# Activation tables loaded at other places, two sums of squares on VectorE, normalised tiles spread over more products, and stores of low parts written one weight later

## The chip, the cores and the metric

One core of one Trainium2 chip runs the whole kernel. The metric is the device time of one launch in microseconds (us), the median of several runs. Its engines are called here as the profile calls them: PE is TensorE (matrix products), DVE is VectorE, ACT is ScalarE, POOL is GpSimd, and SP is SyncE, whose queue issues most of the DMA transfers. Each engine works through its own list of instructions in order.

## The reference, cut to what matters

One layer of a streaming encoder over 1056 frames (1024 of a prompt, 32 of a sample) of 1024 features:

```python
x = x + (sigmoid(ga) * a + sigmoid(gb) * bo) @ w_mix_out      # gated mixers; bo = (...) @ w_conv_out
hc = rms_norm(x, g_cross)
cq = (hc @ w_cq).reshape(B, n, MEM_HEADS, MEM_HEAD_DIM)
s = jnp.einsum('bqhd,bmhd->bhqm', cq, mem_k) * MEM_SCALE
p = jax.nn.softmax(s, axis=-1)
co = jnp.einsum('bhqm,bmhd->bqhd', p, mem_v).reshape(B, n, MEM_DIM)
x = x + co @ w_co
hm = rms_norm(x, g_mlp)
x = x + jnp.square(jax.nn.relu(hm @ w_up)) @ w_down
y = rms_norm(x, g_final)
```

`rms_norm` divides by the root of the mean square of a frame's features, so ACT needs its square root table for each norm and its exponential table for each softmax. Everything is float32.

## The kernel before, in words

**Layout.** Features lie on the 128 partitions in eight blocks (`f` = 0 to 7), frames along the free dimension in three chunks (`CH`): chunk 0 and 1 have 384 frames, chunk 2 has 288. A block of a chunk is one tile.

**Products.** Each float32 operand is split into a high part (rounded, by ACT) and a low part (the rest, by DVE), and a product is the sum of three matmuls: high by high, high by low, low by high (`gemm`, lines 200 to 202; in the MLP lines 885 to 887 and 1817 to 1819). Results collect in PSUM in tiles called `acc`, of which there are three, so a product can start only when the one three before it has been read out. In the MLP's last part another pool of such banks is used, also called `acc` in the profile.

**Weights.** `next_w` hands a product its weight; weights are prepared in the order of `worder`, two ahead (`LOOK`). `fetch_w` (line 159) loads one into `wr`, `issue_w` splits it into `wh` (ACT, line 129) and `wl` (DVE, line 130). Eight weights that serve several chunks are in `kept`: at the first use their low part is stored to DRAM (`wl_d`, line 179), and at later uses it is loaded back (line 172) in place of the DVE split.

**Norms.** `square_acc` squares each tile on ACT (line 279) and adds it to `xacc` on POOL (line 281). `chunk_col` sums over the partitions with matmuls into `pq` (line 232) and finishes on ACT (a square root, line 239) and DVE. `chunk_row` spreads the result over the frames: three products with the identity on ACT and DVE (lines 251 and 252), two matmuls into `pr` (lines 253 and 254), and a copy to `R[c]` on ACT (line 264).

**The middle stage,** about 830 to 1140 us of the span, runs the rest of the mixer, cross-attention and the start of the MLP of different chunks beside each other. For chunk `c`: `do_conv_out(c, f)` eight times (its `acc` read by DVE at line 1073, an addition on POOL at line 1074, a split into `M` tiles by line 129 and 130), `do_mix(c, f)` eight times (each sums over all eight `M` tiles; line 1088 and 285), `do_cq(c, j)` twice (line 1137, and 1141 and 1142 for the queries `Y`), the heads of `Cross` (`scores`: line 1168, exponentials at 1173, division at 1174 and 1176; `turn`: transposes at 1185 and splits into `PTh` and `PTl`; `values`: line 1204 to 1219), and `do_co(c, half)` twice (lines 1231 to 1235). Then `normed(c, f)` makes the MLP's input: a DVE multiply by gain and `R[c]` (line 1310), a store to `xn_d` by SP (line 1313), and for chunk 0 a high part on ACT (line 1321) and a low part on DVE (line 1322).

**Order.** `fillers` is the list of products of chunk 2 and of the first MLP products; `then(i, ...)` puts the steps of the chunk that is one stage on behind filler `i`. Fillers 0 to 7 are `do_conv_out(2, f)`, `do_mix(2, f)` come from 8 on with three `up_one` products between them. From this order a scheduler at build time makes each engine's list, moving instructions by its own estimate of when they can run; what is wrapped in `pin` keeps its order. Loads of ACT's tables are put in where a function of another table comes next in ACT's list.

**The end.** The MLP's last products add into the residual tiles (`to_x1`, line 1801), `squares_of` squares finished tiles, `final(0)` and `final(1)` write the output of the first chunks (line 1842 and 1843), and `final_last(2)` transposes chunk 2 on PE (line 1857), takes `chunk_col(2)` and scales out of PSUM (lines 1872 and 1874).

Of the kernel before, what the change touches and what calls it, by code (L numbers as in the profile page):

```python
# [18 lines left out]
P = 128  # L19
# [21 lines left out]
def hybrid_step(ctx: ExitStack, tc: tile.TileContext, io):  # L41
# [5 lines left out]
    def nm(s):  # L47
        uid[0] += 1
        return f"{s}_{uid[0]}"
# [91 lines left out]
            src = src[j]  # L141
        return src

    fetched = []
    third = {}

    def fetch_w(raw=None):
# [16 lines left out]
    def issue_w(pieces=(slice(0, 1024),)):  # L164
        if not fetched:
            fetch_w()
        raw = fetched.pop(0)
        key = worder[wpos[0]]
        hi = wp.tile([P, 1024], F32R, tag="wh", name=nm("wh"))
        lo = wp.tile([P, 1024], F32R, tag="wl", name=nm("wl"))  # L170
        if kept.get(key) is not None:
            sp.dma_start(lo.bitcast(F32), kept[key])
            act.copy(hi, raw)
        else:
            for at in pieces:
                split(hi[:, at], lo[:, at], raw[:, at])
            if key in kept:
                kept[key] = dram.tile([P, 1024], F32, name=nm("wl_d"))
                sp.dma_start(kept[key], lo.bitcast(F32))
        ready.append((worder[wpos[0]], (hi, lo)))  # L180
        wpos[0] += 1

# [62 lines left out]
    def stats_row(blocks, n, rcol):  # L245

        pr = ps.tile([P, n], F32, tag="pt", bufs=2, name=nm("pr"))
        dh, dl = tmp(n, F32R), tmp(n, F32R)
        for j, b in enumerate(blocks):
            s, r, eye = slice(j * P, b + P), rcol[:, j : j + 1], ident[:, j * P - b :]  # L250
            act.mul(dh[:, s], eye, r)
            dve.scalar_tensor_tensor(dl[:, s], eye, r, dh[:, s].bitcast(F32), op0=ALU.mult, op1=ALU.subtract)
        pe.matmul(pr, ones_r, dh, start=True, stop=False)
        pe.matmul(pr, ones_r, dl, start=False, stop=True)
        return pr
# [2 lines left out]
        RC[c] = misc.tile([P, 3], F32, tag=f"rc{c}", name=nm("rc"))  # L258
        stats_col(accs[c], BLOCKS[c], RC[c], pinned)

    def chunk_row(c):
        n = CH[c][1]
        R[c] = misc.tile([P, n], F32, tag=f"R{c}", name=nm("R"))
        act.copy(R[c], stats_row(BLOCKS[c], n, RC[c]))

    def chunk_stats(c):
        chunk_col(c)
        chunk_row(c)

    def square_acc(x, f, c, on_pool=False):  # L270
        n = CH[c][1]
# [28 lines left out]
    def norm_x():  # L300
# [3 lines left out]
            pe.matmul(acc_tile([P, 384]), spin[:, :P], spin, start=True, stop=True)  # L304
        pool_e.memset(ones, 1.0)
        first_raw = wp.tile([P, 1024], F32, tag="wr", bufs=2, name=nm("wr"))
        warm = misc.tile([P, 1], F32, name="warm")
        with tc.manual_schedule(engines={mybir.EngineType.Activation}):
            act.dma_start(prm, io["params"])
            act.dma_start(first_raw[:, :256], weight(worder[0])[:, :256])  # L310
            act.activation(warm, ones, AF.Sqrt)
        make_identity(nc, ident)
        raws = []

# [814 lines left out]
    def do_cq(c, j):  # L1129
        def fn(w):  # L1130
            n = CH[c][1]
            a = acc_tile([P, n])
            gemm(a, w, xc[c])
            if c == j == 0:
                chunk_row(c)
            t = tmp(n)
            dve.scalar_tensor_tensor(t, a, 0.125, R[c], op0=ALU.mult, op1=ALU.mult)
            for e in range(2):
                own, other = slice(64 * e, 64 * e + 64), slice(64 - 64 * e, 128 - 64 * e)
                q = yslot(c)  # L1140
                act.copy(q[own], t[own])
                dve.tensor_sub(q[other], t[own], q[own].bitcast(F32))
                qc[2 * j + e, c] = q

        return fn
# [106 lines left out]
    def open_first():  # L1252

        closed(m_cm)
        S["l"] = ctx.enter_context(tc.tile_pool(name="first", bufs=4, reuse_waits="tile"))
        S["z"] = ctx.enter_context(tc.tile_pool(name="second", bufs=8, reuse_waits="tile"))
        for f in range(NF):
            z = zslot()
            xa[1][f] = (quarter(z, 0), quarter(z, 1))
            pool_e.dma_start(xa[1][f][1].bitcast(F32)[:, : CH[0][1] - QT], xn_d[:, f, QT : CH[0][1]])  # L1260
        for name in ("w_cq", "w_co"):
            del kept[name, 1]

    def open_sums():
        closed(cr_cm)
# [452 lines left out]
    def then(i, *what):  # L1718
        at.setdefault(i, []).extend(what)
# [1 line left out]
    call = lambda fn, *args: lambda: item(lambda: fn(*args))  # L1721
    assert len(left) == 1
    then(0, *[call(x) for x in left[0][1]])
    then(1, call(chunk_stats, 1))
    then(2, *[lambda j=j: item(do_cq(1, j), ("w_cq", j)) for j in range(2)])
    for f in range(NF):
        then(f // 2, call(normed, 0, f))
    for i, (_, calls) in zip((3, 5, 7, 9, 11, 12), cross_units(1)):
        then(i, *[call(x) for x in calls])
    then(14, lambda: item(do_co(1, 0), ("w_co", 0)))  # L1730
# [6 lines left out]
        then(19 + f // 4, call(normed, 1, f))  # L1737
        then(21 + f // 4, call(second_split, f))
    then(19, call(chunk_col, 2))
    then(20, call(chunk_row, 2))  # L1740
    then(21, lambda: item(do_cq(2, 0), ("w_cq", 0)))
    then(22, lambda: item(do_cq(2, 1), ("w_cq", 1)))
    for i, (_, calls) in zip((23, 25, 26, 28, 29, 31, 32), cross_units(2)):
        then(i, *[call(x) for x in calls])
    then(33, call(open_sums))
    then(34, lambda: item(do_co(2, 0), ("w_co", 0)))
    then(35, lambda: item(do_co(2, 1), ("w_co", 1)))
    for k in range(4):
# [36 lines left out]

    def squares_of(c, x):

        if c == 2 and done[c] == NF - 1:
            sq = tmp(CH[c][1])
            act.activation(sq, x, AF.Square)  # L1790
            accs[c].append(sq)
        else:
            square_acc(x, done[c], c)
        done[c] += 1
# [236 lines left out]
```

## Time and profile before

| | us |
|---|---|
| median of three runs | 1740.44 |
| the three runs | 1740.31, 1743.03, 1740.44 |
| the profiled execution, its own time | 1743.76 |
| span of the profiled execution (first to last instruction) | 1742.0 |
| DVE busy in the span | 1192.8 (68%) |
| ACT busy | 852.9 (49%) |
| POOL busy | 588.0 (34%) |
| mean DMA rate | 199 GB/s |

The span is what the profile covers; the profiled execution's own time is 1.76 us longer than it. In the rows of the profile, a name such as `ct` stands for any tile of that name. "L1073" is line 1073 of the kernel before. "[1.81 <-ACT S L1173]" behind a row says that the engine sat idle for 1.81 us before it, and what ended that. A matmul's record is longer than the spacing of matmuls, since they are pipelined; rows of other engines may also overlap by about 0.1 us. Thirteen table loads stand in ACT's list.

### The profile page before, as it was taken

The page shows a single profiled execution, that of the slowest core. Times are in us where ns is not written, and L with a number is a line of the kernel's source. Part 1 is how long each engine was busy: PE and PEld are TensorE (multiplying, and loading weights), DVE is VectorE, ACT ScalarE, POOL GpSimd, SP SyncE. Part 2 cuts the span into 40 slices and gives each one's busy share as a digit, 9 for nine tenths or more (in the row PEclk, how much of TensorE's full clock was granted, in tenths as well). Part 3 has the DMA queues.
Part 4 walks back from the last instruction along what each step waited for, and adds up shares of the span by engine and source line. Part 5 has one row for each costly group of instructions (what it writes and reads, how often), then busy time and mean ns, then how long its engine had stood idle before and what let it go on. Part 6 is the DMA issues. An engine that isn't in the chain of part 4 may idle for free.

```text
span 1742.0 us, 32567 instructions
## 1 busy us (share of the span) xinstructions
PE 1722.9 (99%) x12238; PEld 1706.9 (98%) x12238; DVE 1192.8 (68%) x2278; ACT 852.9 (49%) x1660; POOL 588.0 (34%) x669
## 2 busy tenths in 40 slices
PE   9999999999999999999999999999999999999998
PEld 8999999999999999999999999999999999999998
DVE  7776776867666756555677888787666686545675
ACT  8653533535335324434556666765444553333443
POOL 0026366453643444442225142106555410000121
PEclk9999999999999999999999999999999999999999
DMA  4333344333435888867766667686666695555554
GB/s 186 103 125 127 117 134 146 121 135 131 159 132 199 296 300 291 290 200 244 265 218 200 223 221 249 222 271 199 214 224 217 218 324 182 193 188 173 189 171 161
DMA packets 179853, 346.60 MB, mean 199 GB/s; under 512 B 18656, under 2 KB 101248, under 8 KB 179568
## 3 DMA queue, kind: packets, MB, share of 16 engines
q1 hardware_dynamic: 163504, 290.07, 50.3%
q0 software_dynamic: 15568, 53.68, 9.0%
q8 instruction: 96, 1.57, 0.4%
q10 hardware_dynamic: 624, 0.77, 0.1%
q14 instruction: 61, 0.50, 0.1%
HBM read 250.73 MB, written 93.14 MB: 197 GB/s over the span
## 4 chain that ended last, share of the span: by engine, by line
PE 55%; DMA 3%; DVE 2%; ACT 1%; issue 1%; POOLq 0%; POOL 0%; DVEq 0%; ACTq 0%; SPq 0%
PE acc L885 6%; PE acc L886 6%; PE acc L887 6%; PE acc L1817 5%; PE acc L1819 5%; PE acc L1818 5%; PE acc L200 4%; PE acc L202 4%; PE acc L201 4%; PE pc L885 2%; PE pc L887 2%; PE pc L886 2%; DMA wr<-wsum_d 1%; DVE wl L130 1%; PE pa L202 1%
## 5 line engine op out<-in xcount | busy, mean ns | idle before, releaser
L129 ACT CAST wh<-wr 128x1024 fp32r<-128x1024 f32 (+1 forms) x214 | 223.8, 1046 | 363.4 <-PE acc L1818 125.5
L130 DVE TENSOR_TENSOR wl<-wr,wh 128x1024 fp32r<-128x1024 f32 (+1 forms) x214 | 277.8, 1298 | 109.5 <-ACT wh L129 108.7
L200 PE MATMUL acc<-X,wh 128*128 128x384 f32 (+1 forms) x864 | 281.4, 326 | 0.0
L201 PE MATMUL acc<-X,wh 128*128 128x384 f32 (+1 forms) x864 | 278.6, 322 | 0.0
L202 PE MATMUL acc<-X,wl 128*128 128x384 f32 (+1 forms) x864 | 277.8, 322 | 0.0
L281 POOL TENSOR_TENSOR xacc<-xacc,ct 128x384 f32<-128x384 f32 (+1 forms) x58 | 77.5, 1339 | 384.6 <-ACT ct L279 382.8
L201 PEld LDWEIGHTS acc<-X,wh 128*128 128x128 f32 x864 | 162.7, 188 | 1.2 <-DVE X L285 0.2
L200 PEld LDWEIGHTS acc<-X,wh 128*128 128x128 f32 x864 | 162.4, 188 | 0.8
L202 PEld LDWEIGHTS acc<-X,wl 128*128 128x128 f32 x864 | 162.4, 188 | 0.1
L200 PE MATMUL acc<-Y,wh 128*128 128x384 f32 (+1 forms) x432 | 139.4, 324 | 3.5 <-DVE ct L1073 3.0
L202 PE MATMUL acc<-Y,wl 128*128 128x384 f32 (+1 forms) x432 | 139.2, 323 | 1.4 <-DMA wl<-wl_d 1.4
L201 PE MATMUL acc<-Y,wh 128*128 128x384 f32 (+1 forms) x432 | 139.1, 322 | 0.0
L129 ACT CAST PTh<-pt 128x512 fp32r<-128x512 f32 (+3 forms) x94 | 45.9, 517 | 113.3 <-PE pt L603 111.5
L1817 PE MATMUL acc<-n,wh 128*128 128x264 f32 x352 | 100.3, 285 | 0.0
L1818 PE MATMUL acc<-n,wh 128*128 128x264 f32 x352 | 100.1, 284 | 0.0
L1819 PE MATMUL acc<-n,wl 128*128 128x264 f32 x352 | 99.9, 284 | 0.0
L740 POOL TENSOR_TENSOR ws<-ws 128x256 f32<-128x256 f32 x100 | 88.7, 887 | 5.6
L740 POOL TENSOR_TENSOR xacc<-xacc 128x256 f32<-128x256 f32 x100 | 87.7, 877 | 5.7 <-DMA xacc<-in_w_in 0.4
L200 PEld LDWEIGHTS acc<-Y,wh 128*128 128x128 f32 x432 | 80.8, 188 | 4.8 <-DVE ct L1073 3.9
L202 PEld LDWEIGHTS acc<-Y,wl 128*128 128x128 f32 x432 | 81.1, 188 | 1.8 <-DMA wl<-wl_d 1.8
L201 PEld LDWEIGHTS acc<-Y,wh 128*128 128x128 f32 x432 | 81.1, 188 | 0.0
L589 ACT ACTIVATE S<-S,nmx 128x257 f32<-128x257 f32 (+1 forms) x132 | 64.2, 488 | 18.9 <-DVE nmx L584 18.5
(433 smaller groups left out, 5544.5 us busy)
## 6 DMA issues: line engine op xcount, KB each, us to landing
wr<-in_w_up SPq DMA_DIRECT2D x53, 512.0 KB, 4.7
wr<-in_w_in SPq DMA_DIRECT2D x52, 512.0 KB, 3.6
wr<-wsum_d SPq DMA_DIRECT2D x40, 512.0 KB, 3.5
wr<-in_w_conv_out SPq DMA_DIRECT2D x24, 512.0 KB, 3.9
wr<-in_w_mix SPq DMA_DIRECT2D x24, 512.0 KB, 4.8
wr<-in_w_down SPq DMA_DIRECT2D x24, 512.0 KB, 3.6
n_d<-Z SPq DMA_DIRECT2D x32, 264.0 KB, 4.1
xacc<-in_w_down POOLq DMA_DIRECT2D x16, 512.0 KB, 4.6
```

Of the source, the lines that this page charges most:

```text
L129: act.copy(hi, src)
L130: dve.tensor_sub(lo, src, hi.bitcast(F32))
L200: pe.matmul(out, wh[:, a], hi, start=(k == 0), stop=False)
L201: pe.matmul(out, wh[:, a], lo, start=False, stop=False)
L202: pe.matmul(out, wl[:, a], hi, start=False, stop=(k == len(acts) - 1))
L740: pin(pool_e.tensor_tensor(t[:, to], t[:, x], t[:, y], op=ALU.add))
L885: pe.matmul(acc, wh[:, a], hi, start=(start and k == 0), stop=False, skip_group_check=True)
L886: pe.matmul(acc, wh[:, a], lo, start=False, stop=False, skip_group_check=True)
L887: pe.matmul(acc, wl[:, a], hi, start=False, stop=(k == 3), skip_group_check=True)
L1817: pe.matmul(a, wh[:, s], hi, start=(t == 0 and k == 0), stop=False, skip_group_check=True)
L1818: pe.matmul(a, wh[:, s], lo, start=False, stop=False, skip_group_check=True)
L1819: pe.matmul(a, wl[:, s], hi, start=False, stop=(t == 1 and k == 7), skip_group_check=True)
```

## The change

1. **Tables.** `chunk_row` can take a table: behind the copy of `R[c]` ACT runs one dummy activation of one column with scale 0 into `warm`, so that the load of the exponential table stands there and not ahead of the first softmax of that chunk's cross-attention. This is done for all three chunks. `root_table`, called at filler 33 behind `open_sums`, does the same with the square root once the last exponential of chunk 2 is over; it reads the last attention tile, so it comes behind its writing. The number of table loads stays thirteen.
2. **Last squares.** In `squares_of`, the squares of the last two finished tiles of chunk 2 go into tiles of their own on ACT. The first is appended to the list of sums, and DVE adds the second to it. Before, only the last had its own tile, and POOL added the one ahead of it to `xacc`.
3. **Normalised tiles.** `normed(0, f)` stood at fillers 0 to 3, two at each; it now stands at fillers 1 to 8, one at each.
4. **Stores.** The store of a kept weight's low part is written in the code when the next weight is issued (list `leaving`), not at once.

```diff
@@ issue_w
         hi = wp.tile([P, 1024], F32R, tag="wh", name=nm("wh"))
         lo = wp.tile([P, 1024], F32R, tag="wl", name=nm("wl"))
+        for to, at in leaving:
+            sp.dma_start(to, at.bitcast(F32))
+        leaving.clear()
...
                 kept[key] = dram.tile([P, 1024], F32, name=nm("wl_d"))
-                sp.dma_start(kept[key], lo.bitcast(F32))
+                leaving.append((kept[key], lo))
...
-    def chunk_row(c):
+    warm = []
+
+    def chunk_row(c, table=None):
         n = CH[c][1]
         R[c] = misc.tile([P, n], F32, tag=f"R{c}", name=nm("R"))
         act.copy(R[c], stats_row(BLOCKS[c], n, RC[c]))
+        if table:
+            act.activation(warm[0], R[c][:, :1], table, scale=0.0)
...
             if c == j == 0:
-                chunk_row(c)
+                chunk_row(c, AF.Exp)
...
+    def root_table():
+        act.activation(warm[0], co[2][1][0][:, :1].bitcast(F32), AF.Sqrt, scale=0.0)
...
-    then(1, call(chunk_stats, 1))
+    then(1, call(chunk_stats, 1, AF.Exp))
...
     for f in range(NF):
-        then(f // 2, call(normed, 0, f))
+        then(1 + f, call(normed, 0, f))
...
-    then(20, call(chunk_row, 2))
+    then(20, call(chunk_row, 2, AF.Exp))
...
-    then(33, call(open_sums))
+    then(33, call(open_sums), call(root_table))
...
     def squares_of(c, x):
 
-        if c == 2 and done[c] == NF - 1:
+        if c == 2 and done[c] >= NF - 2:
             sq = tmp(CH[c][1])
             act.activation(sq, x, AF.Square)
-            accs[c].append(sq)
+            if done[c] == NF - 2:
+                accs[c].append(sq)
+            else:
+                dve.tensor_add(accs[c][1], accs[c][1], sq)
```

Lines of the kernel after the change are 3 to 13 higher than before.

**DVE, from the norm of chunk 0 to the first normalised tiles.** The rows are DVE's list behind the `rc` of chunk 0; `ct` from `acc` and `Ga` is the reading of a `do_conv_out(2, f)` product, `ct` from `Ga`, `prm` and `R` is the first half of a `normed`, `Y` from `ct` its second half. Before:

```order
L252 SCALAR_TENSOR_TENSOR ct_11242<-ident,rc_11224,ct_11241 128x128 x3
L130 TENSOR_TENSOR wl_11391<-wr_2080_11388,wh_11390 128x1024
L238 TENSOR_SCALAR st_v_11311<-pq_11307 128x3
L1310 SCALAR_TENSOR_TENSOR ct_11252<-Ga_1703_9819,prm,R_11239 128x384
L240 RECIPROCAL st_y_11313<-st_s_11312 128x3
L241 TENSOR_TENSOR st_t_11314<-st_v_11311,st_y_11313 128x3
L242 SCALAR_TENSOR_TENSOR st_t_11314<-st_t_11314,st_y_11313 128x3
L1322 TENSOR_TENSOR Y_2044_11256<-ct_11252,Y_2043_11255 128x264
L1310 SCALAR_TENSOR_TENSOR ct_11259<-Ga_1715_9868,prm,R_11239 128x384
L1073 TENSOR_TENSOR ct_11299<-acc_11274,Ga_1385_8179 128x288
```

Now, at the same place:

```order
L255 SCALAR_TENSOR_TENSOR ct_11243<-ident,rc_11225,ct_11242 128x128
L1080 TENSOR_TENSOR ct_11286<-acc_11261,Ga_1385_8179 128x288
L255 SCALAR_TENSOR_TENSOR ct_11243<-ident,rc_11225,ct_11242 128x128 x2
L130 TENSOR_TENSOR wl_11372<-wr_2071_11369,wh_11371 128x1024
L241 TENSOR_SCALAR st_v_11298<-pq_11294 128x3
L130 TENSOR_TENSOR M_11290<-ct_11286,M_11289 128x288
L243 RECIPROCAL st_y_11300<-st_s_11299 128x3
```

The reading of the second `do_conv_out` product (from `Ga_1385`) was the tenth of these rows and is the second; the first normalised tile has moved behind the whole norm of chunk 1.

**ACT, about the last table load of the middle stage.** `lt` from `acc` is the reading of an `up` product, `Y` and `h` from `tO` the end of the last attention head, `n` and `t` from `ct` are casts of MLP operands, `st_s` the root. Before, the two places read:

```order
L1213 CAST Y_2458_13049<-tO_13425 64x256
L1218 CAST h_2541_13429<-tO_13425 64x256
L1385 ACTIVATE lt_13599<-acc_13522 128x264
L129 CAST wh_13552<-wr_2581_13550 128x1024
```

```order
L1404 CAST t_2545_13468<-ct_13729 128x240
L1404 CAST n_2553_13479<-ct_13730 128x240
L239 ACT_TABLE_LOAD
L239 ACTIVATE st_s_13757<-st_v_13756 128x3
L1385 ACTIVATE lt_13767<-acc_13700 128x264
```

Now:

```order
L1220 CAST Y_2458_13052<-tO_13428 64x256
L1225 CAST h_2541_13432<-tO_13428 64x256
L1272 ACT_TABLE_LOAD
L1272 ACTIVATE warm<-Y_2458_13052 128x1
L1395 ACTIVATE lt_13603<-acc_13526 128x264
L129 CAST wh_13556<-wr_2581_13554 128x1024
```

```order
L1414 CAST t_2545_13471<-ct_13733 128x240
L1414 CAST n_2553_13479<-ct_13734 128x240
L242 ACTIVATE st_s_13761<-st_v_13760 128x3
L1395 ACTIVATE lt_13771<-acc_13704 128x264
```

The load has left the place ahead of the root and stands, with the dummy, 22 rows earlier, ahead of another reading of an `up` product.

**SP, about a store of a low part.** `wl_d` from `wl` is the store, `wl` from `wl_d` a load of another low part, `wr` the loads of weights. Before:

```order
L179 DMA wl_d_10275<-wl_10272 128x1024
L159 DMA wr_10402<-in_w_conv_out 128x1024
L159 DMA wr_10461<-in_w_conv_out 128x1024
L159 DMA wr_1862_10501<-in_w_mix 128x1024
L1069 DMA ct_10408<-m_d_93 128x384
L159 DMA wr_10576<-in_w_mix 128x1024
L172 DMA wl_10464<-wl_d_9596 128x1024
```

Now:

```order
L172 DMA wl_d_10275<-wl_10272 128x1024
L159 DMA wr_10403<-in_w_conv_out 128x1024
L159 DMA wr_10462<-in_w_conv_out 128x1024
L159 DMA wr_1862_10502<-in_w_mix 128x1024
L1076 DMA ct_10409<-m_d_93 128x384
L159 DMA wr_10577<-in_w_mix 128x1024
L175 DMA wl_10465<-wl_d_9596 128x1024
```

Nothing has moved but line numbers and names; the same holds of all eight stores, and of SP's whole list up to the second `do_conv_out` of chunk 2.

More of the change, by code (lines that the diff above doesn't have):

```diff
@@ L142, in weight @@
         return src
-    fetched = []
+    fetched, leaving = [], []
     third = {}
@@ L264, in chunk_row, with chunk_stats @@
         act.copy(R[c], stats_row(BLOCKS[c], n, RC[c]))
-    def chunk_stats(c):
+        if table:
+            act.activation(warm[0], R[c][:, :1], table, scale=0.0)
+    def chunk_stats(c, table=None):
         chunk_col(c)
-        chunk_row(c)
+        chunk_row(c, table)
     def square_acc(x, f, c, on_pool=False):
@@ L306, in norm_x @@
         first_raw = wp.tile([P, 1024], F32, tag="wr", bufs=2, name=nm("wr"))
-        warm = misc.tile([P, 1], F32, name="warm")
+        warm.append(misc.tile([P, 1], F32, name="warm"))
         with tc.manual_schedule(engines={mybir.EngineType.Activation}):
@@ L310, in norm_x @@
             act.dma_start(first_raw[:, :256], weight(worder[0])[:, :256])
-            act.activation(warm, ones, AF.Sqrt)
+            act.activation(warm[0], ones, AF.Sqrt)
         make_identity(nc, ident)
@@ L1134, in fn @@
             if c == j == 0:
-                chunk_row(c)
+                chunk_row(c, AF.Exp)
             t = tmp(n)
```

## The prediction

> **What bounds the kernel now.** First the page's opening rows (engine, busy us, share of the span, instructions), then PE's waits: the engine, what it was to write and at which line, what released it, and total, times and longest.
>
> ```profile
> span 1742.0 us, 32567 instructions
> PE 1722.9 (99%) x12238; PEld 1706.9 (98%) x12238; DVE 1192.8 (68%) x2278; ACT 852.9 (49%) x1660; POOL 588.0 (34%) x669
> ...
> PE acc L200 <- DVE ct L1073: 3.0, 3, 1.5
> PE acc L886 <- DVE Z L1328: 1.8, 2, 0.9
> PE acc L202 <- DMA wl<-wl_d: 1.4, 1, 1.4
> PE acc L304 <- DVE ct L302: 1.3, 1, 1.3
> PE acc L885 <- ACT lt L1385: 1.2, 1, 1.2
> PE pq L232 <- POOL xacc L281: 0.9, 1, 0.9
> PE acc L885 <- DVE Gb L1235: 0.8, 1, 0.8
> ```
>
> PE is busy 99% of the span and the change takes no product away. So the stake is PE's idle time, and these seven rows make 10.4 us of it: no step can win more than its own row. Four touch the change: the three waits for line 1073 (a bank `acc` that DVE reads late), the wait for the low part from `wl_d`, the wait for `lt` at line 1385, and the wait for POOL's last addition. A second sort of loss shows in the windows (stretch, its length, busy us and count of PE, PEld, DVE, ACT and POOL, granted clock, DMA share and rate):
>
> ```profile
> 1074.00:1076.00 2.00, 2.00 (x11) 2.00 (x10) 1.87 (x5) 1.22 (x3) 0.00 (x0) 0.50 0.52 189
> ...
> 1078.00:1080.00 2.00, 2.00 (x19) 2.00 (x18) 1.57 (x5) 2.00 (x5) 0.00 (x0) 1.00 0.00 0
> ```
>
> PE counts as busy in both, but at a clock of 0.50 it gets 11 matmuls done instead of 19. Eight matmuls in 2 us are some 0.8 us; the whole dip, about twice as long, I estimate at 1.7. It stands right behind the two waits for line 1328.
>
> **The change part by part: stores.** All eight stores stay at the same row of SP's list, as the order rows show, so the wait for `wl_d` (1.4) stays: 0. Bounds 0 and 0.
>
> **The square root's load.** Before, ACT did this:
>
> ```profile
> 1119.51 0.39 ACT L1385 ACTIVATE lt<-acc 128x264 f32<-128x264 f32 x1 [0.29 <-PE acc L887]
> 1120.85 1.05 ACT L129 CAST wh<-wr 128x1024 fp32r<-128x1024 f32 x1 [0.95 <-PE acc L886]
> ...
> 1135.46 1.28 ACT L239 ACT_TABLE_LOAD   x1
> 1136.75 0.20 ACT L239 ACTIVATE st_s<-st_v 128x3 f32<-128x3 f32 x1
> 1136.87 0.37 ACT L1385 ACTIVATE lt<-acc 128x264 f32<-128x264 f32 x1
> ```
>
> The load held back `lt`, and PE waited 1.2 for it. Without it `lt` is 1.28 earlier and the wait goes. What is late next is the `lt` of 1119.51: 1.28 for the load and 0.20 for a dummy stand ahead of it. ACT idles 0.29 and 0.95 there, so 1.48 − 1.24 = 0.24 us reach the `wh` behind it, which is prepared ahead. I take 1.1 of the 1.2. Bounds: 0, if PE waits as long for the delayed `lt`, and 1.2.
>
> The Trainium skill, "ScalarE: Activation LUTs", section "What ACT_TABLE_LOAD costs", puts a switch at a load of 1283 ns and a drain of 1380 ns. The 1.28 agrees, but here the next instruction starts 0.01 us behind the load's end, with no drain; by the page this gain would shrink by up to 1.4. The rows decide.
>
> **Tables for the softmax.** Chunk 0's load moves from about 894 to 887 us, where PE has no wait: 0, bounds 0 and −0.2 for the dummy. Chunk 1's belongs to the next part. Chunk 2's moves from 1083.91, where PE doesn't wait either, to behind the first of the three casts here:
>
> ```profile
> 1071.12 1.04 ACT L1327 CAST Z<-Z 128x264 fp32r<-128x264 f32 x3
> ...
> 1072.87 1.11 DVE L1328 TENSOR_TENSOR Z<-Z 128x264 fp32r<-128x264 f32 x3
> ```
>
> The second cast then ends 1.48 later, at about 1073.3, and DVE's low part of it, 0.43 long, at 1073.8. Before, that low part was the second of the lower row, ending at about 1073.6. PE lives on these tiles, so I charge −0.2; bounds 0 and −1.5, the whole load and dummy, if nothing covers it.
>
> **Normalised tiles and the cross stage.** This is the largest term.
>
> ```profile
> 990.53 0.17 DVE L1174 RECIPROCAL rec<-den 128x3 f32<-128x3 f32 x1 [1.81 <-ACT S L1173]
> 990.74 0.88 DVE L1176 TENSOR_SCALAR S<-S,rec 128x256 f32<-128x256 f32 x3
> 991.54 1.22 DVE L130 TENSOR_TENSOR wl<-wr,wh 128x1024 fp32r<-128x1024 f32 x1
> 992.67 0.42 DVE L1322 TENSOR_TENSOR Y<-ct,Y 128x264 fp32r<-128x264 f32 x1
> 993.02 0.61 DVE L1310 SCALAR_TENSOR_TENSOR ct<-Gb,prm,R 128x384 f32<-128x384 f32 x1
> 993.55 0.81 DVE L1073 TENSOR_TENSOR ct<-acc,Gb 128x288 f32<-128x288 f32 x2
> ```
>
> DVE stood still for 1.81 us because ACT loaded its table first:
>
> ```profile
> 987.73 1.28 ACT L1173 ACT_TABLE_LOAD   x1
> 989.02 0.47 ACT L1173 ACTIVATE S<-sc,nmx 128x256 f32<-128x256 f32 x1
> ```
>
> Then it did a low part and two rows of normalised tiles ahead of the reading that PE waited for. The change takes out both reasons: the load goes to about 976, and six of the eight normalised tiles go from 972–996 to about 995–1025. The rows of DVE from 960 to 1035 (busy us and mean ns) give their weight, and the windows the room:
>
> ```profile
> L1322 DVE TENSOR_TENSOR Y<-ct,Y 128x264 fp32r<-128x264 f32 x8 | 4.9, 607 | 0.1
> ...
> L1310 DVE SCALAR_TENSOR_TENSOR ct<-Gb,prm,R 128x384 f32<-128x384 f32 x5 | 3.1, 613 | 0.0
> ...
> L1310 DVE SCALAR_TENSOR_TENSOR ct<-Ga,prm,R 128x384 f32<-128x384 f32 x3 | 1.8, 611 | 0.2 <-ACT R L264 0.2
> ```
>
> ```profile
> 970.00:980.00 10.00, 8.44 (x51) 7.79 (x50) 9.43 (x22) 5.62 (x13) 1.91 (x2) 1.00 0.62 205
> 980.00:990.00 10.00, 10.00 (x79) 10.00 (x78) 8.26 (x14) 7.64 (x16) 0.81 (x1) 1.00 0.66 218
> 990.00:1000.00 10.00, 8.52 (x66) 8.29 (x65) 9.43 (x22) 7.68 (x20) 2.44 (x3) 1.00 0.89 291
> 1000.00:1010.00 10.00, 10.00 (x81) 9.98 (x80) 8.97 (x18) 7.47 (x18) 2.55 (x3) 1.00 0.51 156
> 1010.00:1020.00 10.00, 10.00 (x79) 10.00 (x78) 9.90 (x20) 8.12 (x18) 3.07 (x3) 1.00 0.64 213
> 1020.00:1030.00 10.00, 10.00 (x69) 9.86 (x68) 7.85 (x15) 6.45 (x12) 4.86 (x5) 1.00 0.87 282
> ```
>
> Eight tiles cost 4.9 + 3.1 + 1.8 = 9.8 us, six 7.35. DVE is idle for 0.57 + 1.74 + 0.57 = 2.88 us from 970 to 1000 and for 1.03 + 0.10 + 2.15 = 3.28 from 1000 to 1030. So the three waits can go, all 3.05 (1.56 missing from PE in the first slice, 1.48 in the third, whose sum is 3.04), but the work lands where DVE is 90 to 99% busy. PE stays ahead of its old place only as far as DVE, which empties its banks, gets ahead too, and DVE gains only the idle time it gives up. By 1020 the same work has to be done, and the two slices in which the tiles land hold 1.03 + 0.10 = 1.13. I take **1.1** of the 3.05, because the tight slice 1010–1020 (9.90 of 10) is the nearest row. Upper bound 3.05, if the idle time of 970 to 1000 is given up too. Lower bound: 7.35 in 3.28 leaves 4.07 of new waits, less 3.05: −1.0. The wait for line 1235 (0.8) behind it stays.
>
> **The last squares.** The end of the kernel:
>
> ```profile
> 1730.51 1.90 POOL L281 TENSOR_TENSOR xacc<-xacc,ct 128x288 f32<-128x288 f32 x2 [13.13 <-ACT ct L279]
> ...
> 1731.74 0.43 ACT L1790 ACTIVATE ct<-Gb 128x288 f32<-128x288 f32 x1
> ...
> 1732.46 0.83 PE L232 MATMUL pq<-ones,xacc 128*128 128x1 f32 x6 [0.93 <-POOL xacc L281]
> ...
> 1733.15 0.81 PE L232 MATMUL pq<-ones,ct 128*128 128x1 f32 x6
> ```
>
> PE's sums began at 1732.46, held by POOL's second addition (0.95 us each). That addition goes, and DVE gets one; on DVE such a tile takes 0.45 (the two readings of line 1073 above are 0.81 for two). It can start when ACT's last square is done, at 1732.17, so the second set of sums starts at about 1732.7 instead of 1733.15, and the first set fits ahead of it. Gain 0.45, taken as **0.4**; bounds 0 and 0.9, the whole wait.
>
> **Sum.** 0 + 1.1 + 0 − 0.2 + 1.1 + 0.4 = 2.4 us. The profiled execution took 1743.76 (span 1742.0 and 1.76 around it), which gives 1741.4. It is 3.3 over the median of the three runs, 1740.44; nearly all of the 2.4 hangs on waits that any run should have, so I take the same from the median: **1738.0**.
>
> **The rivals.** *Full recovery:* DVE's own idle time from 970 to 1000 absorbs the load's 1.28, the tiles are spread so thin that no bank is late, and the whole 3.05 stays: 3.05 + 1.1 + 0.4 − 0.2 = 4.35, or 1736.1; with the last wait whole, 1735.6. For it: a spare 1.81 us on DVE just ahead of the worst wait. Against it: 9.90 of 10.
>
> *DVE becomes the bound (slower):* the six tiles push DVE past its room between 1000 and 1030, 4.07 us of readings come late, PE waits for `acc` there and the clock falls behind it, as it did behind the waits at 1068 to 1072. 1740.44 + 4.07 − 3.05 + 1.7 − 1.5 + 0.2 = 1741.9; with the full 1.5 for chunk 2's load 1743.2. It decides from 4.35 us of new waits and lost clock in that stretch. For it: 3.28 against 7.35; against it: the tiles can slip beyond 1030, since PE needs them only in the MLP.
>
> The Trainium skill, "TensorE: Matmul & The Clock Gate", section "What's actually happening", halves the clock only after an idle window of some 3.4 us. The dip here follows waits of 0.9 us, so by the rule there would be no dip in any case, and the 1.7 would drop out of this rival.
>
> *The change does not do what it says:* the stage is bound by DVE's total, the waits only move, and chunk 1's load buys nothing: 1.1 + 0.4 − 0.2 = 1.3, or 1739.1. It also covers the stores, which already do nothing.
>
> **How the numbers follow.** Chances: forecast 0.46 (own range 1737.0 to 1739.9, with the unknown 0 to 1.2 of the root's load and half a microsecond of the cross stage), full recovery 0.30, DVE the bound 0.13, no effect in the stage 0.11. About 0.2%, 3.5 us, is what a measurement of this kernel can tell from no change: faster is below 1736.96, slower above 1743.92. Full recovery lies below it nearly throughout (0.27), with the low edge of the forecast (0.06): faster 0.33. Slower is the upper half of the DVE case: 0.06. The rest, 0.61, is the same. Range 1734.8 to 1742.0: below, full recovery with some of the 1.7 of the clock back; above, the DVE case; it leaves out the ends of these two, about 0.2.
>
> **What would show it.** The last root load stands near 1119 and no wait for `lt` at 1136 is left. In the waits line 1073 falls from 3.0 to below 0.5; if that total appears again at other names (`acc` behind line 1088 or 1235, `M`) between 1000 and 1040, the forecast's mechanism is right, and if nothing appears, full recovery. DVE's slices from 1000 to 1030 rise towards 10. The wait for `Z` at 1068 to 1072 grows by less than 0.5, and the wait for `wl_d` stays at 1.4. The first `pq` on `xacc` starts without a wait, the last near 1732.7 in old time. Wrong would be: new waits of over 1 us at places that this text doesn't name, or a clock dip gone or doubled, which would shift the sum by 1.7 either way.

## The result, and the profile after

The change makes the kernel slower. Its median is 1746.91 us (12 runs, 1741.56 to 1751.34), that of the kernel before 1740.38 on the same chip (12 runs, 1737.22 to 1747.33). The ratio is 1.0029, with an interval of 1.0017 to 1.0041: 5.0 us lost, 3.0 to 7.1, where 2.4 gained were forecast and 1742.0 was the end of the range.

The profiled execution of the changed kernel took 1742.62, 4.3 less than its own median. First the page's opening rows, then PE's waits (engine, what it was to write and at which line, what released it, total, times, longest):

```profile
span 1740.8 us, 32568 instructions
PE 1723.7 (99%) x12238; PEld 1706.7 (98%) x12238; DVE 1193.3 (69%) x2279; ACT 853.5 (49%) x1664; POOL 590.0 (34%) x668
...
PE acc L203 <- DVE uh L1368: 1.6, 1, 1.6
...
PE acc L893 <- DVE Z L1338: 1.2, 2, 0.9
...
PE acc L1238 <- DVE Gb L1095: 0.8, 1, 0.8
...
PE acc L892 <- DVE Ga L1095: 0.6, 1, 0.6
...
PE acc L205 <- DVE wl L130: 0.5, 1, 0.5
PE acc L892 <- ACT lt L1395: 0.5, 1, 0.5
PE acc L892 <- DVE Gb L1242: 0.4, 1, 0.4
PE acc L203 <- DVE ct L1080: 0.4, 1, 0.4
```

Line 1073 is now line 1080, and its 3.0 us are 0.4. The rows for the low part from `wl_d` and for POOL's last addition are gone, and so is the wait for `lt` behind the table load; the 0.5 for `lt` that is listed is another one, at 1164 us. In their place stand waits that weren't there: `uh` (1.6), `Ga` and `Gb` behind line 1095, `wl`. The largest is explained by DVE's rows ahead of it (start, length, what, and in brackets how long DVE stood and for what):

```profile
1013.43 0.43 DVE L1332 TENSOR_TENSOR Y<-ct,Y 128x264 fp32r<-128x264 f32 x1
1014.86 1.23 DVE L130 TENSOR_TENSOR wl<-wr,wh 128x1024 fp32r<-128x1024 f32 x1 [0.99 <-ACT wh L129]
1016.00 0.43 DVE L1368 TENSOR_TENSOR uh<-acc,us 128x264 f32<-128x264 f32 x1
```

The bank that PE needs is read in the last row, behind the low part of the last moved tile (the first row) and behind a `wl` for which DVE itself stood 0.99 us.

An execution that is 4.3 below its median shows little of a loss of 5.0, so here is a second one (the run "change again" below): 1747.30, span 1745.5. Its waits from 970 to 1050 us:

```profile
PE acc L203 <- DVE uh L1368: 1.6, 1, 1.6
PE acc L1238 <- DVE Gb L1095: 1.3, 1, 1.3
PE acc L892 <- DVE Ga L1095: 1.0, 1, 1.0
PE o L1211 <- DVE tO L1214: 0.8, 1, 0.8
PE acc L203 <- ACT M L129: 0.7, 1, 0.7
PE acc L203 <- DVE ct L1144: 0.6, 1, 0.6
PE acc L205 <- DVE wl L130: 0.5, 1, 0.5
```

With two of 0.4 behind them they make 7.3 us. Before, the same stretch had two rows, 3.0 and 0.8.

To place the loss I cut each trace by its matmuls, which are counted alike in every kernel here. Between the 6000th and the 6500th matmul (about 950 to 1025 us) lie, at full clock, 72.8 us before, 75.5 and 77.4 in the two executions of the change. From the 7000th to the 7450th the change gains 1.4 (56.8 to 55.4), from the 7450th to the 7800th it loses 0.7 (43.8 to 44.6). The rest is alike within what two executions of one kernel differ by, the waits for weights between the 5500th and 6000th above all.

### The profile page after: what moved, and what is told of

It is laid out like the page before. It is cut to its first block, busy times and chain, and to the rows that moved or that the text cites. A ratio compares the mean times of both kernels' runs of the same rounds, so it can differ in the third digit from the quotient of the medians.

```text
span 1740.8 us, 32568 instructions
## 1 busy us (share of the span) xinstructions
PE 1723.7 (99%) x12238; PEld 1706.7 (98%) x12238; DVE 1193.3 (69%) x2279; ACT 853.5 (49%) x1664; POOL 590.0 (34%) x668
## 4 chain that ended last, share of the span: by engine, by line
PE 91%; DMA 3%; DVE 3%; ACT 2%; issue 1%; SPq 0%; POOL 0%; DVEq 0%; POOLq 0%; ACTq 0%
PE acc L203 13%; PE acc L205 13%; PE acc L204 13%; PE acc L892 6%; PE acc L893 6%; PE acc L894 6%; PE acc L1832 6%; PE acc L1830 6%; PE acc L1831 6%; PE pc L892 2%; PE pc L894 2%; PE pc L893 2%; PE pt L610 2%; PE sc L585 1%; PE sc L584 1%
## 5 line engine op out<-in xcount | busy, mean ns | idle before, releaser
L288 POOL TENSOR_TENSOR xacc<-xacc,ct 128x384 f32<-128x384 f32 (+1 forms) x57 | 78.5, 1382 | 377.3 <-ACT ct L286 375.5
```

## The experiments

**How the table is read.** All kernels were timed in turn with the kernel before on the same chip, 5 to 12 runs each; "us" is the ratio less 1 times that kernel's median, with the ends of its interval. "Stage" is the time from the 6000th to the 6500th matmul in the run's profile, with half of its half-clock time taken off. "Last M" is the time from the 6000th matmul to the start of the last low part of chunk 2's tiles `M`. These eight pairs `M` are what the first mixer product of chunk 2 sums over, so PE can't end that product without the last one; whether PE came to stand for it is read from its waits. Each comes from a `do_conv_out(2, f)`: SP loads an addend (`ct` from `m_d`), PE makes a product, DVE reads it, the addend is added, ACT and DVE split the sum.

| kernel | median | us against before | stage | last M |
|---|---|---|---|---|
| before | 1740.4 | 0 | 72.8 | 54.8 |
| change; again (e4) | 1746.9; 1747.1 | +5.0 (3.0, 7.1); +4.9 (1.7, 8.0) | 75.5; 77.4 | 58.5; 59.9 |
| e1 tables alone | 1740.5 | −2.3 (−5.2, 0.9) | 71.3 | 53.7 |
| e2 tiles alone | 1749.4 | +7.7 (4.7, 10.6) | 78.1 | 60.7 |
| e3 squares alone | 1742.5 | −0.2 (−3.1, 2.6) | 73.4 | 54.8 |
| e5 e2, PE's old list | 1750.3 | +7.8 (5.1, 10.6) | 76.8 | 58.3 |
| e6 before, PE's new list | 1751.6 | +7.8 (5.4, 10.3) | 78.1 | 57.5 |
| e7 all but the tiles | 1739.2 | −3.0 (−5.2, −0.9) | 71.4 | 54.4 |
| e8 change, PE's old list | 1745.3 | +4.0 (1.7, 6.1) | 76.0 | 57.0 |
| e9, e10, e11: addend's own place in e2, before, e7 | 1749.0, 1748.2, 1749.6 | +7.0, +5.9, +6.4 | 77.5, 75.4, 75.8 | 58.4, 59.6, 59.2 |
| e12, e13: stores on ACT's queue in e2, before | 1750.2, 1746.0 | +8.0, +4.4 | 77.6, 76.3 | 62.5, 55.6 |
| e14, e15: both edits in e2; change with stores on ACT's queue | 1748.7, 1746.3 | +7.1, +4.7 | 78.5, 75.5 | 58.0, 58.7 |
| e16 before, more work on DVE | 1743.5 | +2.8 (1.0, 4.5) | 74.4 | 55.0 |
| e17 before, later addends | 1747.4 | +5.4 (2.4, 8.4) | 76.4 | 59.3 |
| e18 e1, earlier addends | 1737.9 | −3.8 (−5.9, −1.7) | 72.0 | 54.1 |

**One part at a time.** e1 has the four dummies and nothing else of the change, e3 the squares, e4 is the change again, and e2 has one line:

```diff
     for f in range(NF):
-        then(f // 2, call(normed, 0, f))
+        then(1 + f, call(normed, 0, f))
```

The tables:

> Only the tables are loaded ahead (three exponential loads, one root load); PE's, DVE's and POOL's lists are those of before. Theory A (the move of the normalised tiles is what costs the 6.5 us between the medians): faster by 1 to 2 us, the wait for lt at 1136 (1.2) gone. Theory B (a load that now stands behind a copy of R stops casts that PE lives on): slower by 3 to 6 us, with new waits for Z or for M near 975, 1072 or 1119.

The tiles:

> Only the normalised tiles are spread over eight products; the tables, the last squares and the stores are as before. Theory A: slower by 5 to 8 us, with new waits of PE between 1000 and 1045 that together exceed the 3.05 us saved at line 1073. Theory B: within 1.5 us of before.

The squares:

> Only the squares of the last two tiles are changed. Both theories: 0.4 us faster, which the interval can't tell from nothing; the wait for POOL's addition (0.9) is gone from PE's waits. A third theory, that the tail itself costs several us, would show as slower by over 3 us with a later last output.

The change again:

> The changed kernel once more, for a second look: its first profiled execution took 1742.62, 4.3 below the median of its runs, 1746.91, so the first trace shows little of the loss. Theory A: the median is again 4 to 7 us over before, and a profile nearer to that median has more PE waits between 1000 and 1045 than the 4.7 us of the first (1.6 behind line 1368 among them). A rival, C: the waits are the same and the clock falls more often; then the excess is in stretches of clock 0.50.

The tiles alone lose 7.7 us, and the other parts show no loss. The later run e7 is the change with that one line undone, and its 0.9983 against the change's 1.0029 prices the line at 0.0046, 8.0 us. Two ways, one answer: the loss is the line that moves `normed`.

**PE's list.** Moving the tiles also turns the order of products on PE. A list can be held by edges that set an order and no wait (the numbers are places in the program's list of matmuls, most of the pairs are left out). In the trace of e17 below, which holds four lists so, those of PE, DVE, ACT and POOL are row by row those of before.

```diff
+    PE_ORDER = [(6047, 6071), (6076, 6112), (6045, 6046), (6071, 6073), ...
+    seq = [mm[i] for a, b in PE_ORDER for i in range(a, b)]
+    for i, j in zip(seq, seq[1:]):
+        tc.add_manual_dep(j, i.name, mybir.DependencyInfo(mybir.DependencyClass.NoSync, ...
```

e5 is e2 and e8 the change with PE's list of before; e6 is the kernel before with PE's list of e2; e7 is told above.

> The normalised tiles are spread as in e2, but PE's list is held, matmul by matmul, to that of before; DVE, ACT and SP still get their six tiles later. Theory A1 (the loss of e2, 7.6 us, comes from PE's new list, which sends the heads and the mixer products close behind what they depend on): within 2 us of before, the waits for uh, tO and M between 1000 and 1030 gone. Theory A2 (the loss comes from DVE's work, 7.35 us of it, landing between 1000 and 1030): 5 to 8 us slower, with PE waiting for DVE's readings there.

> The reverse: the normalised tiles stay at two a product as in before, and PE's list alone is that of e2. A1: 5 to 8 us slower, with the waits for uh (1.6), tO (0.8) and M (about 1) of e2 and e4. A2: within 2 us of before.

> The change without its third part: tables, last squares and stores; PE's list is that of before. By e1 (0.9987) and e3 (0.9999): faster by 1.5 to 3 us. If the tables cost something that only the moved tiles cover, it would be slower than e1.

> The whole change with PE's list held to that of before. A1: 2 to 5 us faster than before (the tables and whatever the freed DVE time at 970 to 1000 gives). A2: 3 to 6 us slower, as the change itself.

With PE's old list the moved tiles still cost 7.8 us, so undoing PE's order alone wins nothing back. What PE waits for then is above all the tile `M`; the waits of e5 from 975 to 1050:

```profile
PE acc L200 <- ACT M L129: 3.1, 2, 2.0
PE acc L885 <- ACT Y L1321: 1.1, 1, 1.1
PE acc L200 <- DVE ct L1137: 1.0, 1, 1.0
...
```

(and 0.6 at two others). The equal totals hide a difference, though. In e5 and e6 the granted clock is lower (mean over the runs 0.9955 and 0.9953, against 0.9981 of the kernel before beside them), which makes 4.5 and 4.9 us of their 1750; in e8 (0.9965 against 0.9981) some 2.8 of its 4.0. In e2 it makes only 0.9 (0.9974 against 0.9979), and in the change none (0.9980 against 0.9979). So with PE's old list the waits cost less and the clock more, and that PE's new order costs nothing in e2 isn't shown.

e6 has the old place of the tiles with PE's new list, and is as bad: in one gap of 5.7 us PE waits for a reading of line 1073. It isn't PE's list alone, as its expectation has it: the scheduler turned the other lists too, 100 of DVE's 2278 rows and 22 of SP's 943 in the trace. So these runs don't part PE's order from the rest, and the next question is why `M` is late.

**The buffer of the addends.** The addends and the moved tiles take turns on the same six `ct` buffers. Here the addend of chunk 2 goes straight into the place that the low part of `M` takes later, so it needs no `ct`; e9 is e2 with it, e10 the kernel before, e11 the kernel e7, each with PE's list held.

```diff
-            t1 = tmp(n)
+            if c == 2:
+                lo = mslot(n)
+                t1 = lo.bitcast(F32)
+            else:
+                t1 = tmp(n)
...
-            mg[c][f] = (mslot(n), mslot(n))
+            mg[c][f] = (mslot(n), lo if c == 2 else mslot(n))
```

> The normalised tiles spread as in e2, with e2's PE list, but the addend of the chunk 2 products (the load from m_d) goes straight into the tile that later holds the low part of M, and no longer into one of the six ct tiles that the normalised tiles use too. Theory S (e2's loss comes from the shared ct tiles: a normalised tile holds one until its store is over, the load of the addend starts late, the last M tile comes 3 to 6 us later and the first mixer product with it): at least 5 of the 7.6 us come back, and the last M tile is done by 56 us behind the stage's 6000th matmul (54.8 before, 60.7 in e2). Theory A2 (DVE's 7.35 us of work lands where it has no room): 5 to 8 us slower as e2, since DVE does the same work at the same places.

> Control for e9: the kernel before with its PE list, and the addend loaded into the M tile in the same way. Theory S: 0 to 3 us faster (the loads wait little there); theory A2: within 1.5 us. A slower time than before would say that the M tile is a worse place for the load, and by how much e9 has to be read down.

> The change without its third part (e7, 0.9983), with the addend loaded into the M tile, PE's list that of before. If S holds and e10 is not slower: 3 to 5 us faster than before, the fastest so far. If not: as e7, about 3 us faster.

The moved kernel doesn't recover (7.0 against 7.7), and the two controls, which should have stayed as they were, lose 5.9 and 9.4 (e7 to e11). The edit makes the last `M` late by itself, 59.6 and 59.2 instead of 54.8 and 54.4; that the place for `M` comes free late too is a guess. It also turned the other lists (44 of SP's rows, 19 of DVE's and 11 of ACT's in e10). As a test of the buffers this failed. It counts for the chain of `M` only so far: PE's one new wait in the two controls is for `M`, 3.2 and 3.7 us, and by the mean clock (0.9967 and 0.9958 against 0.9982) 2.6 and 4.2 us of their losses are clock.

**The queue of the stores.** Each `normed` of chunk 0 stores its tile (`xn_d` from `ct`) on SP, and what stands behind a store on SP waits for DVE to make the tile. Here the eight stores go on ACT's queue, in e2 (e12), before (e13), e2 with the edit of e9 (e14) and in the change (e15).

```diff
-            sp.dma_start(xn_d[:, f, o : o + n], t)
+            (sp if c else act).dma_start(xn_d[:, f, o : o + n], t)
```

> As e2 (tiles spread, same PE list), but the eight stores of chunk 0's normalised tiles are issued from ACT's queue, not SP's; SP's list is otherwise that of e2. Theory Q (SP works in order: a store that waits for a late normalised tile holds up the addend's load from m_d and the weight loads behind it; in e2, e4, e5 and e9 the last such load starts 0.4 us behind the sixth store): at least 4 of the 7.6 us come back, SP's waits for ct at the store's line (13.0 us between 975 and 1012 in e2) are gone, the last addend load starts 3 us or more earlier. Theory A2 (the work on DVE itself): 5 to 8 us slower, as e2. Theory S' (the ct tile is what the load waits for, on whatever queue): as e2 too.

> Control for e12: the kernel before, PE's list held, with the same stores on ACT's queue. Q: 0 to 3 us faster (SP waited 9.5 us for those tiles there too). A2 and S': within 2 us.

> e12 with the addend loaded into the M tile as in e9, so that neither SP's queue nor a ct tile ties the addend to the normalised tiles. Q: as e12. S' together with Q: clearly faster than e12, within 2 us of before. A2: still 5 to 8 us slower, and then DVE's work itself is the cause.

> The whole change with those stores on ACT's queue, all lists as the scheduler makes them. Q: 0 to 4 us faster than before, as the tables and squares of e7 (0.9983) come on top of e12. A2 and S': 3 to 6 us slower, as the change itself (1.0028).

Nothing is won back (8.0 against 7.7, 4.7 against 5.0), and the control loses 4.4. This doesn't clear SP's queue, since the sums aren't early in e12 either. One takes 7.3 us to land there, and the last `M` is the latest of all, 62.5; in e13 SP stands 5.2 us at the addends for a buffer (`ct` from the store). The three controls of these two sets (e10, e11, e13) add no work and cost 4.4 to 9.4 us; DVE's list is turned in each of them, by 19 to 32 rows.

**Work without delay, delay without work.** The last pair parts the two theories that were left: DVE has too much to do, or the addends, and with them `M`, come late. In e16 all four lists of PE, DVE, ACT and SP are those of before, the tiles stay, and twelve idle reductions are put on DVE where e2 has its last six tiles:

```diff
+    def more_work():
+        for _ in range(2):
+            extra.append(dve.tensor_reduce(spare, R[0], axis=AX.X, op=ALU.max).ins)
...
+    for f in range(2, NF):
+        then(1 + f, call(more_work))
```

In e17 nothing is added. The lists of PE, DVE, ACT and POOL are those of before; on SP the loads of the fifth to seventh addend of chunk 2 stand behind a load of a low part, the eighth store and two loads of weights.

> The kernel before with the lists of PE, DVE, ACT and SP held, and only work added on DVE: twelve reductions of 128x384 into a spare column, some 5 to 6 us, each at the count of other DVE instructions at which e2 does a multiply or a low part of a moved tile. No ct tile, store or load is touched. They do nothing for the result. Theory A2 (DVE's work between 995 and 1025 costs the time by itself): 4 to 7 us slower. Theory L (the loss comes from the chain of chunk 2's M tiles, whose readings and addend loads were put behind the moved tiles by list, queue and ct tile): at most 2 us slower, the last M tile within 1.5 us of before.

> The kernel before with the lists of PE, DVE, ACT and POOL held, and only three addend loads from m_d (the fifth to the seventh of chunk 2) moved on SP's queue, behind a load of a low part, the eighth store and two weight loads that they stood ahead of. Theory L: the fifth and sixth M tile come 3 to 5 us later and PE waits for M at the first mixer product; 1.5 to 5 us slower. Theory A2: within 1 us, since DVE's work is as before.

First the added work in e16, then two of its windows (stretch, length, busy us and count of PE, PEld, DVE, ACT and POOL, clock, DMA share and rate):

```profile
L1312 DVE TENSOR_REDUCE spare<-R x12: 514/539/552, 987.2 to 1015.6; 128x1 f32<-128x384 f32 x12
1000.00:1010.00 10.00, 10.00 (x81) 9.98 (x80) 10.00 (x22) 8.18 (x20) 2.99 (x3) 1.00 0.56 175
1010.00:1020.00 10.00, 9.31 (x69) 8.90 (x68) 9.90 (x22) 6.52 (x15) 2.23 (x2) 1.00 0.42 138
```

Twelve of 539 ns are 6.5 us, against the 7.35 of the six tiles. DVE is full for 20 us on end, and PE loses 0.7 us there. The whole costs 2.8 us (1.0 to 4.5), about a third of e2; that is less than the one theory forecast (4 to 7) and more than the other (at most 2). The change's own windows for the same stretch say it the other way round:

```profile
1000.00:1010.00 10.00, 8.87 (x63) 8.35 (x64) 9.77 (x24) 7.84 (x25) 0.93 (x1) 1.00 0.32 100
1010.00:1020.00 10.00, 7.87 (x54) 7.07 (x54) 8.66 (x18) 6.76 (x13) 1.58 (x1) 1.00 0.71 229
```

(second execution): PE misses 1.1 and 2.1 us, the more where DVE has 1.3 us to spare.

e17 costs 5.4 us (2.4 to 8.4) with no work added and DVE's list untouched. Its largest waits from 945 to 1055 (line 1073 had 3.0 before), and ACT's row ahead of the `S` in question:

```profile
PE acc L200 <- DVE ct L1073: 3.3, 3, 1.9
PE sc L1168 <- ACT S L1173: 3.1, 1, 3.1
...
1002.36 0.43 ACT L129 CAST M<-ct 128x288 fp32r<-128x288 f32 x1 [6.03 <-POOL ct L1074]
```

The loss doesn't come by the way that was expected: PE doesn't wait for `M` at the mixer product. ACT's list has the high part of the fifth tile `M` ahead of a head's exponentials (line 1173). ACT stands 6.03 us for the sum that the late addend goes into, the exponentials come late, and PE stands 3.1 us for them at the next head's scores. A stretch of 3.41 us at half clock follows at 1004.0, which costs 1.7. With 0.3 more at line 1073 that is nearly all of the 5.3 us by which this stage is longer than before with the clock left in (78.1 against 72.8).

The addends are as late in e2. SP's rows about the addends in the kernel before (start and length of issuing, x2 for two in a row):

```profile
985.92 3.16 SPq L1313 DMA_DIRECT2D xn_d<-ct  x2
989.17 0.86 SPq L1069 DMA_DIRECT2D ct<-m_d  x2
991.24 0.32 SPq L172 DMA_DIRECT2D wl<-wl_d  x1
993.45 0.32 SPq L1069 DMA_DIRECT2D ct<-m_d  x1
993.87 0.38 SPq L1313 DMA_DIRECT2D xn_d<-ct  x1
994.30 0.94 SPq L159 DMA_DIRECT2D wr<-in_w_mix  x2
995.73 0.33 SPq L1069 DMA_DIRECT2D ct<-m_d  x1
```

and with the tiles alone moved (e2):

```profile
987.22 0.33 SPq L1313 DMA_DIRECT2D xn_d<-ct  x1
987.59 0.43 SPq L1069 DMA_DIRECT2D ct<-m_d  x1
990.01 0.32 SPq L1313 DMA_DIRECT2D xn_d<-ct  x1
...
994.94 0.38 SPq L1069 DMA_DIRECT2D ct<-m_d  x1
996.53 0.33 SPq L1313 DMA_DIRECT2D xn_d<-ct  x1
1000.34 0.33 SPq L159 DMA_DIRECT2D wr<-in_w_up  x1
1000.77 0.38 SPq L1069 DMA_DIRECT2D ct<-m_d  x1
1003.24 0.32 SPq L1313 DMA_DIRECT2D xn_d<-ct  x1
1003.66 0.37 SPq L1069 DMA_DIRECT2D ct<-m_d  x1
```

Before, the last addend leaves at 995.73; now every one of the last four stands behind a store of a moved tile, for which SP waits for DVE, and the last leaves at 1003.66. The stores aren't all of it: the last two also stand behind a load of weights for `up` (1000.34), which before came behind them all, and ahead of which SP stands 3.41 us for DVE's `wl`. From 978 to 1004 us SP stands 5.4 us at the stores in e2, where it was 7.0 before, and 10.4 us for `wl` at loads of weights, where it was 1.9. Counted from the 6000th matmul, which e2 reaches 2.1 us later, that is 46.7 and 52.5, 5.8 us later; in the change's two executions 50.7 and 51.7, in e17 52.4.

**Can more be had?** e18 has the tables of e1 and moves the seventh addend on SP ahead of a load of a low part and the eighth ahead of two loads of weights, with the lists of PE and DVE as before.

> The reverse of e17 on top of e1: tables loaded ahead, the lists of PE and DVE those of before, and on SP's queue the seventh addend load moved ahead of a load of a low part and the eighth ahead of two weight loads. Theory L: the last M tile 1 to 3 us earlier than in e7 (54.4), 2 to 4 us faster than before, at or below e1 (0.9987) and e7 (0.9983). If PE's wait for the first mixer product is gone already in e1 and e7, then as they are, and no more is to be had here; a slower time would say that the weights moved back are missed sooner.

At 1737.93 it is the fastest of all, 0.9978 (0.9966 to 0.9990), but its last `M` is not earlier than in e1 or e7 (54.1, 53.7, 54.4) and its interval overlaps theirs. Its gain can't be told from that of the tables; that earlier addends add to it isn't shown.

## Why the prediction was wrong, step by step

**Stores: right.** SP's rows for the eight stores are where they were. The wait for `wl_d`, which was to stay at 1.4, is absent in the first execution of the change and 1.4 in the second; over all traces it goes from none to 2.8, so it tells nothing.

**The square root's load: right, and a little more.** ACT after the change:

```profile
1118.54 1.28 ACT L1272 ACT_TABLE_LOAD   x1
1119.83 0.20 ACT L1272 ACTIVATE warm<-Y 128x1 f32<-128x1 f32 x1
1119.94 0.37 ACT L1395 ACTIVATE lt<-acc 128x264 f32<-128x264 f32 x1
1120.50 1.05 ACT L129 CAST wh<-wr 128x1024 fp32r<-128x1024 f32 x1 [0.18 <-PE acc L893]
...
1135.00 0.20 ACT L242 ACTIVATE st_s<-st_v 128x3 f32<-128x3 f32 x1
```

The load stands at 1118.54, the wait for `lt` at 1136 is gone, and `wh` isn't late. The stretch from the 7000th to the 7450th matmul is 55.4 in every kernel with the four dummies and 56.8 in every one without: 1.4 where 1.1 was taken, over the bound of 1.2 by a little. The Trainium skill, "ScalarE: Activation LUTs", section "What ACT_TABLE_LOAD costs", adds a drain of 1380 ns to a load; here the next instruction follows 0.01 us behind the load, and the gain is whole.

**Tables for the softmax: right, and worth more alone.** In e7 the exponential's load of chunk 1 stands at 978.06, and DVE's wait ahead of the reciprocal is 0.39 instead of 1.81:

```profile
989.11 0.17 DVE L1181 RECIPROCAL rec<-den 128x3 f32<-128x3 f32 x1 [0.39 <-ACT S L1180]
```

The third of the waits for line 1073, the 1.48 behind that load, is gone, and the stage is 71.3 and 71.4 instead of 72.8: 1.4 to 1.5, which the prediction had folded into the 1.1 of the next term. Chunk 2's load cost nothing that shows: the waits for `Z` on DVE are 0.9 to 1.6 in executions with the dummies and 0.9 to 1.8 without.

**The last squares: not to be measured.** Alone 0.9999 (0.9982 to 1.0015). The wait of 0.93 for POOL is gone in the change, and 0.06 for DVE's addition stands in its place. But in executions without the edit the wait for POOL goes from none (e1, e2, e17) to 1.9 us (e5), so the size stays open within a microsecond or two.

**Normalised tiles and the cross stage: this step failed.** The prediction gave this term a gain of 1.1, with a loss of 1.0 as its lower bound. Its own run, e2, loses 7.7 (4.7 to 10.6). The step weighed DVE's work against DVE's idle time and nothing else: it counted a moved tile as its two instructions on DVE, and the prediction held that "the tiles can slip beyond 1030, since PE needs them only in the MLP". Two things were left out of the sum.

The first is that each tile also takes a `ct` buffer and puts a store on SP, that SP's list is turned with it, so that addends of chunk 2 stand behind these stores and behind a load of weights, and that the readings of those products move in DVE's list. The last addend goes out 4 to 6 us later, and the last `M` is ready 4 to 6 us later.

The second is that the first product of the MLP stands in this very stage. Before, its 24 matmuls ran from 1005.4 to 1010.9, and the last tile was done at 996.0. In the change's first execution they run from 1003.9 to 1014.9, and the last tile is done at 1013.9, just ahead of the matmuls that read it:

```profile
1014.36 0.28 PE L892 MATMUL acc<-Y,wh 128*128 128x264 f32 x1
...
1016.48 0.40 PE L203 MATMUL acc<-M,wh 128*128 128x288 f32 x1 [1.59 <-DVE uh L1368]
```

`uh` reads the bank of that product, and PE's wait for it is the largest of the stage in both executions of the change and in e2. With PE's old list (e5, e8) PE waits 1.1 for the high part of a moved tile itself.

The delay of the addends alone, with every other list as before, costs 5.4 (e17); more work alone costs 2.8 (e16). The sum, 8.2, is near the 7.7, but intervals this wide allow that and don't prove it. PE's own waits in e2 are not those of e17 either: of the 6.5 us that it stands between the 6000th and the 6500th matmul (3.0 before), 1.1 is for `M`, and most of the rest for late readings by DVE, `uh` with 1.6 first. So it is shown that the line costs the 7.7, that late addends can cost most of such a sum by themselves, and that added work on DVE with the lists of before costs less (1.0 to 4.5); how much of e2's loss comes by the addends is argued, and no run undoes the late first product of the MLP alone.

The signs that the prediction named were half right. Line 1073 fell below 0.5, and its total appeared again at other names, as the forecast's mechanism had it; but in the second execution these (`Ga` and `Gb` behind line 1095, `Gb` behind 1242, `M`) had 3.4 of the 7.3 us. Of the other 3.9, 0.4 is what is left of line 1073, and 3.5 stood at places that the text didn't name, `uh` with 1.6 first: by its own words, a wait of over 1 us at such a place is the sign of a wrong prediction. DVE's busy time in the slices from 1000 to 1030 didn't rise throughout: 8.97, 9.90 and 7.85 before, 9.90, 8.53 and 6.91 in the first execution, 9.77, 8.66 and 9.02 in the second.

**The rivals.** "DVE becomes the bound" had the right sign at 0.13, and the wrong mechanism for most of it: e16 fills DVE and pays a third. "Full recovery" and "does not do what it says" fell. The chance for slower, 0.06, was far too low since every rival drew on the same row, DVE's idle time.

**What stays open.** How the lateness divides among SP's queue, the `ct` buffers and DVE's list: removing one of the three left or made another (e9 to e15), and all three at once was not tried. DVE's new list without its new work was not tried either. The loss of 0.7 between the 7450th and 7800th matmul goes with the moved tiles and with PE's new list (e6). 0.48 of it is one wait of PE for a reading `lt`, at 1164 us in the change's first execution, which every kernel with that loss has and no other; why `lt` is late there is open.

## What to carry to other kernels

A step that is moved takes along its buffers and its DMAs: before its compute is weighed against an engine's idle time, look at how the order of the queue changes with it and which loads come to stand behind its stores, at what stands behind them in every engine's list, and at where the first product stands that reads the moved result. Test such a case by delaying only the loads and by adding only the work, with all other lists held. And take a second profile before reading a difference of 0.3% from one.

## What the runs showed of the hardware that was not expected

**A long dip of the clock behind a short gap.** In e10 PE stood 2.1 us, from about 1002.3, and the clock fell at 1004.2 and stayed at half for 10.2:

```profile
1002.00:1004.00 2.00, 0.26 (x2) 0.03 (x1) 0.98 (x2) 0.08 (x1) 0.79 (x1) 1.00 0.74 250
1004.00:1006.00 2.00, 1.60 (x6) 1.38 (x7) 0.96 (x2) 1.97 (x7) 0.00 (x0) 0.55 0.59 193
...
1012.00:1014.00 2.00, 2.00 (x11) 2.00 (x10) 0.00 (x0) 0.00 (x0) 0.00 (x0) 0.50 0.00 0
```

Up to 1700 us of each trace (the end of the span aside), the granted clock was low for 3.41, 6.83 or 10.24 us, one, two or three times the same length. The Trainium skill, "TensorE: Matmul & The Clock Gate", section "What's actually happening", has a window of that length; that a whole window must be idle does not hold here: PE had stood for 1.9 us when the clock fell.

**The same gap with and without a dip.** The prediction saw a dip at 1074 behind waits of 0.9 us. The change has such a wait for `Z` in both of its executions, 0.91 us at 1072.43 and at 1075.53. In the first the clock behind it stays whole:

```profile
1074.00:1076.00 2.00, 2.00 (x16) 1.93 (x16) 1.84 (x6) 1.93 (x7) 0.00 (x0) 1.00 0.88 291
```

In the second it falls:

```profile
1078.00:1080.00 2.00, 2.00 (x12) 2.00 (x10) 1.69 (x5) 1.88 (x6) 0.00 (x0) 0.50 0.58 227
```

No dip follows the longer wait of 1.59 us for `uh` in either execution. So the 1.7 us of a dip comes and goes between executions of one kernel, and is no fixed term of a sum; over many runs it can differ between kernels, as the mean clock of e5 and e6 shows.

**The spread.** One kernel's runs lie 10 us apart (1737.22 to 1747.33 before), twice the effect in question, so a single execution of each can't tell two of these kernels apart.
